# The last LayerNorm of a hybrid decoder layer: two engines on row block 6, the variance constant on DVE, the last store on ACT's queue

## The chip, the cores and the metric

The kernel runs on one core of one Trainium2 chip. The metric is device time in microseconds (us), median of three runs. The engines are called as the profile calls them: PE (matmul; PEld is its weight load), DVE (vector), ACT (scalar), POOL (GpSimd) and SP, which issues most DMAs. A "q" behind a name (SPq, POOLq) is the engine's instruction queue: DMA issues, semaphores, drains.

## What is computed

One decoder layer in float32 on 1024 rows of width 1024. Its end, on which the change bears most, is

```python
h = layer_norm(DEEPNORM_ALPHA * h + mix, ln1_g[l], ln1_b[l])
h = layer_norm(DEEPNORM_ALPHA * h + memory_cross_attention(h, mem, ...), ln2_g[l], ln2_b[l])
h = layer_norm(DEEPNORM_ALPHA * h + swiglu_ffn(h, ffn_w_gate_up[l], ffn_w_down[l]), ln3_g[l], ln3_b[l])
```

with `layer_norm` being, per row, `(x - mean) * rsqrt(var + 1e-5) * g + b`. `mix` is the output of an S5 state-space group and a differential attention group.

## The kernel before, in words

The 1024 rows are eight row blocks of 128 rows, one block being a tile `u` of 128 partitions by 1024 columns. Most matmuls are done as three in a rounded format (`fp32r`), on a high and a low part of each operand; making these parts costs ACT and DVE much work along the whole kernel. The stages follow each other: input LayerNorm and projections, S5, attention, output projection with the first LayerNorm (`project`, eight blocks), cross attention with the second LayerNorm (`project` again, eight blocks, woven with the last of the cross attention), the gate and up product (`gate_up`), and the down product (`down`).

Statistics of these three LayerNorms come from `ln_stats` (line 310), called 24 times, eight times per LayerNorm. Two `bn_stats` and one `bn_aggr` on DVE give mean and variance (tile `bmv`). Line 317 adds the constant 1e-5 to the variance on POOL (tile `bv`). Line 307 takes the power -0.5 of that on POOL (tile `lny`). The caller then goes on, on DVE.

`project` (line 1088) normalises its block on DVE, and `resid` (line 320) does two 128x1024 products and sums of the block on POOL, back to back, and stores the result.

`down` (line 1402) works in two halves of four row blocks. Blocks 0 to 3 are finished while PE works on the second half. For blocks 4 to 7 the last five of the 22 steps of the sum are done block by block and half by half, and each half of 512 columns is added to the residual on DVE (`stt`, reading PSUM). The PSUM tiles are, in the order of the blocks, `sc`, `sc`, `mm`, `tp`: the tile `tp` is block 7. After each block comes `tail(ti, z, fast)` (line 1426) with `fast` being 0, 2, 1, 2 for blocks 4, 5, 6, 7:

- `fast` 0 (block 4): a small DVE instruction makes `nm`, ACT normalises the block, DVE multiplies with `g3`, POOL adds `b3`, POOL's queue stores.
- `fast` 1 (block 6): the same, but DVE also adds `b3`, and SP's queue stores.
- `fast` 2 (blocks 5 and 7): no ACT. For each half of columns DVE does `(z - mean) * g3`, which needs only `bmv`, then `z * rstd + b3`, which needs `lny`, and SP's queue stores the half.

The order of each engine's instructions is not written out by hand: the framework's planner takes instructions by priority (place in the program) and by a simulated time line, and each engine then runs its list in order. At the end of the program (line 1617) each engine drains, SP waits for all transfers and engines, and a barrier ends the run.

The trace puts nearly all instructions on line 120, that of a helper, so they are told apart by tile names.

Of the kernel before, what the change touches and what calls it, by code (L numbers as in the profile page):

```python
# [12 lines left out]
ALU = mybir.AluOpType  # L13
# [12 lines left out]
EPS = 1e-5  # L26
# [66 lines left out]
def layer(ctx: ExitStack, tc: tile.TileContext, a, out, dbg=None):  # L93
# [55 lines left out]
    sc_e, ve, po, pe, sy = (Eng(getattr(nc, n), n) for n in ("scalar", "vector", "gpsimd", "tensor", "sync"))  # L149
# [22 lines left out]
    def U(shape=(128, 1024), dt=F32):  # L172
        return alloc("u", 1024, shape, dt)

    def H(shape=(128, 512), dt=F32):
        return alloc("h", 512, shape, dt)

    def fr_(*ts_):
        for t in ts_:
            if isinstance(t, (tuple, list)):  # L180
                fr_(*t)
            else:
                _, tag, nm, slot = held.pop(id(t))
                free[tag].append((slot, used.pop(nm), cur[0], icnt[0], last.get(nm, 0)))
# [19 lines left out]
    def S(w, name, dt=F32):  # L204
        return sm.tile([128, w], dt, tag=name, name=name)
# [7 lines left out]
    def act(o, i, scale=1.0, bias=0.0, func=None, accum=None):  # L213
        f = func or (AF.Copy if isinstance(bias, float) and bias == 0.0 else AF.Identity)
        kw = {}
        if not (isinstance(bias, float) and bias == 0.0):
            kw["bias"] = bias
        if accum is not None:
            kw["accum_out"] = accum
        return sc_e.activation(out=o, in_=i, func=f, scale=scale, **kw)  # L220

    def tt(e, o, x, y, op):
        return e.tensor_tensor(out=o, in0=x, in1=y, op=op)

    def ts(e, o, x, s1, op0, s2=None, op1=None):
        if op1 is None:
            return e.tensor_scalar(out=o, in0=x, scalar1=s1, scalar2=None, op0=op0)
        return e.tensor_scalar(out=o, in0=x, scalar1=s1, scalar2=s2, op0=op0, op1=op1)

    def stt(o, x, s, y, op0, op1):  # L230
        return ve.scalar_tensor_tensor(out=o, in0=x, scalar=s, in1=y, op0=op0, op1=op1)
# [5 lines left out]
    def lo_of(o, x, hi, e=None):  # L237
        return tt(e or ve, o, x, hi.bitcast(F32), ALU.subtract)
# [16 lines left out]
    def load(ap, shape=(128, 1024)):  # L255
        t = U(shape)
        sy.dma_start(out=t, in_=ap)
        return t
# [4 lines left out]
    def wload(ap, shape=(128, 1024), e=None, eh=None):  # L263
        raw = load(ap, shape)
        w = split(raw, shape, None, e, eh)
        fr_(raw)
        return w
# [37 lines left out]
    def rsqrt(v, w, nm):  # L305
        y = S(w, nm + "y")
        tt(po, y, v, half_[:, 0:w], ALU.pow)
        return y

    def ln_stats(z):  # L310
        st = S(12, "bst")
        for c in range(2):
            ve.bn_stats(out=st[:, 6 * c:6 * c + 6], in_=z[:, 512 * c:512 * c + 512])
        mv = S(2, "bmv")
        ve.bn_aggr(out=mv, in_=st)
        v = S(1, "bv")
        ts(po, v, mv[:, 1:2], EPS, ALU.add)
        return mv[:, 0:1], rsqrt(v, 1, "ln")

    def resid(z, g, b, dst):  # L320
# [6 lines left out]
    def row_bc(n):  # L327
        t = U()
        ap = a["rows"]
        sy.dma_start(out=t, in_=bass.AP(tensor=ap.tensor, offset=ap.offset + n * DM, ap=[[0, 128], [1, DM]]))  # L330
        return t
# [756 lines left out]
    def project(src, wname, r_idx, grow, gn, bn, hT, r_out, at=None):  # L1088
# [4 lines left out]
        for i in range(NT):  # L1093
# [14 lines left out]
            if i == NT - 1:  # L1108
                fr_(w)
            mean, rstd = ln_stats(z)  # L1110
            ts(ve, z, z, mean, ALU.subtract, rstd, ALU.mult)
            resid(z, g, b, r_dram[r_out][i])
# [289 lines left out]
    def down():  # L1402
        g3, b3 = row_bc(6), row_bc(7)
        bk = [x[:, 512 * c:512 * c + 512] for x in banks["sc"] for c in range(2)] + banks["mm"] + banks["tp"]
        tails = []

        def prep(half, j):
            w = wload(a["wdown"][j])
            hx = U([128, 2, 512], F32R)
            v = H()  # L1410
            sy.dma_start(out=v, in_=hid_dram[j, half])
            act(hx[:, 0, :], v)
            lo_of(hx[:, 1, :], v, hx[:, 0, :])
            fr_(v)
            return w, hx

        def go(j, w, hx, i, cs=(0, 1)):
            s = slice(128 * i, 128 * i + 128)
            for c in cs:
                n = slice(512 * c, 512 * c + 512)  # L1420
                o = bk[2 * i + c]
                pe.matmul(o, lhsT=hx[:, 0, s], rhs=w[0][:, n], start=(j == 0), stop=False)
                pe.matmul(o, lhsT=hx[:, 0, s], rhs=w[1][:, n], start=False, stop=False)
                pe.matmul(o, lhsT=hx[:, 1, s], rhs=w[0][:, n], start=False, stop=(j == NJ - 1))

        def tail(ti, z, fast=0):
            mean, rstd = ln_stats(z)
            if fast < 2:
                nm = S(1, "nm3")
                stt(nm, mean, -1.0, rstd, ALU.mult, ALU.mult)  # L1430
                act(z, z, scale=rstd, bias=nm)
                tt(ve, z, z, g3, ALU.mult)
                tt(ve if fast else po, z, z, b3, ALU.add)
                (sy if fast else po).dma_start(out=out[128 * ti:128 * ti + 128, :], in_=z)
                fr_(z)
                return
            for c in range(2):
                n = slice(512 * c, 512 * c + 512)
                stt(z[:, n], z[:, n], mean, g3[:, n], ALU.subtract, ALU.mult)
                stt(z[:, n], z[:, n], rstd, b3[:, n], ALU.mult, ALU.add)  # L1440
                sy.dma_start(out=out[128 * ti:128 * ti + 128, n], in_=z[:, n])
            fr_(z)

        ahead = [prep(0, j) for j in range(DD)]
        for half in range(2):
            for j in range(NJ - LAST):
                w, hx = ahead.pop(0)
                if j + DD < NJ - LAST:
                    ahead.append(prep(half, j + DD))
                for i in range(4):  # L1450
                    go(j, w, hx, i)
                fr_(w, hx)
                if tails and j % 3 == 2:
                    tail(*tails.pop(0))
            zs = [load(r_dram[2][4 * half])]
            last = [prep(half, j) for j in range(NJ - LAST, NJ)]
            if half == 0:
                ahead = [prep(1, j) for j in range(DD)]
            for i in range(4):
                ti = 4 * half + i  # L1460
                if i < 3:
                    zs.append(load(r_dram[2][ti + 1]))
                z = zs[i]
                for c in range(2):
                    for jj in range(LAST):
                        go(NJ - LAST + jj, last[jj][0], last[jj][1], i, (c,))
                    n = slice(512 * c, 512 * c + 512)
                    stt(z[:, n], z[:, n], ALPHA, bk[2 * i + c], ALU.mult, ALU.add)
                if half == 0:
                    tails.append((ti, z))  # L1470
                else:
                    tail(ti, z, (0, TA, 1, 2)[i])
            fr_(last)
# [147 lines left out]
```

## Time and profile before

| what | value |
|---|---|
| three runs | 1528.99, 1529.14, 1533.43 us; median 1529.14 |
| profiled execution | 1530.15 us, span 1528.4 us |
| PE busy | 1424.2 us (93%), 7246 matmuls |
| DVE busy | 918.2 us (60%), 1507 instructions |
| ACT busy | 526.8 us (34%) |
| POOL busy | 494.3 us (32%) |
| mean granted PE clock | 0.972 of full |

The span is the time from the first to the last instruction in the trace; 1.75 us of the profiled execution lie outside of it. The shares are averages over stages with different limits. In the last slice of the page (the last 38 us) PE is busy for six tenths and POOL for nearly none.

### The profile page before, as it was taken

To read this page: it belongs to the slowest core of one execution; us is meant where nothing else is said; L and a number is where in the kernel's file an instruction comes from. 1 tells how busy PE (TensorE), PEld (TensorE's weight loads), DVE (VectorE), ACT (ScalarE), POOL (GpSimd) and SP (SyncE) were. 2 spreads that over 40 slices of the span, in tenths; PEclk is the share of its full clock that TensorE was granted. 3 is DMA by queue.
4 is the path that set the end of the run, shared out by engine and by line. 5 is a ranking of instruction groups with operands and counts; after the bars stand their busy time and mean duration, and the time that the engine had idled before them with its cause. 6 is when DMAs were issued, how large, how long until landed. Compare 5 with 4: busy or idle time off the path is not lost.

```text
span 1528.4 us, 18806 instructions
## 1 busy us (share of the span) xinstructions
PE 1424.2 (93%) x7246; PEld 1201.2 (79%) x7246; DVE 918.2 (60%) x1507; ACT 526.8 (34%) x926; POOL 494.3 (32%) x414
## 2 busy tenths in 40 slices
PE   7988779999896999999999899999999999999996
PEld 6988668878776788888887678878888887888885
DVE  8896665566785465635557856656555547337305
ACT  5411214655774012425212533323323326324200
POOL 4344431132004766000255645534444420004002
PEclk9999889999998899999999999999999999999998
DMA  9104361221337124124222223312222249554401
GB/s 343 68 1 97 75 159 42 56 56 51 116 101 285 42 69 153 48 76 129 93 83 83 97 90 117 111 69 84 89 83 82 84 148 330 190 185 146 152 28 55
DMA packets 53870, 166.82 MB, mean 109 GB/s; under 512 B 6346, under 2 KB 10863, under 8 KB 53780
## 3 DMA queue, kind: packets, MB, share of 16 engines
q1 hardware_dynamic: 41652, 124.17, 24.7%
q0 software_dynamic: 9232, 30.94, 5.9%
q10 hardware_dynamic: 2896, 10.51, 2.7%
q8 instruction: 57, 0.93, 0.3%
q14 instruction: 33, 0.27, 0.1%
HBM read 126.77 MB, written 34.62 MB: 106 GB/s over the span
## 4 chain that ended last, share of the span: by engine, by line
PE 63%; DVE 13%; DMA 10%; issue 5%; POOL 4%; ACT 3%; SPq 0%; ACTq 0%; POOLq 0%; DVEq 0%
PE mm L120 33%; PE sc L120 23%; DVE u L120 11%; PE tp L120 7%; POOL u L120 3%; ACT u L120 3%; DMA u<-in_wgu_dram 2%; DMA kr<-u 2%; DMA u<-in_x_dram 1%; DMA u<-in_wkvv_dram 1%; DVE h L120 1%; DMA u<-kr 1%; DMA hidd<-u 1%; DMA u<-in_wqk_dram 1%; ACT h L120 1%
## 5 line engine op out<-in xcount | busy, mean ns | idle before, releaser
L120 PE MATMUL mm<-u,u 128*128 128x512 f32 (+1 forms) x3288 | 729.1, 372 | 34.5 <-ACT u L120 19.7
L120 PEld LDWEIGHTS mm<-u,u 128*128 128x128 f32 x3288 | 570.4, 192 | 140.6 <-ACT u L120 22.2
L120 PE MATMUL sc<-u,u 128*128 128x512 f32 (+4 forms) x2744 | 598.6, 375 | 25.6 <-DVE u L120 8.1
L120 PEld LDWEIGHTS sc<-u,u 128*128 128x128 f32 (+2 forms) x2744 | 482.6, 200 | 114.6 <-ACT u L120 10.8
L120 DVE TENSOR_TENSOR u<-u,u 128x1024 fp32r<-128x1024 f32 (+5 forms) x257 | 317.2, 1253 | 209.1 <-ACT u L120 171.6
L120 ACT ACTIVATE u<-u 128x1024 fp32r<-128x1024 f32 (+1 forms) x200 | 195.0, 985 | 467.8 <-DMA u<-in_wgu_dram 118.5
L120 POOL TENSOR_TENSOR u<-u,u 128x512 f32<-128x512 f32 (+4 forms) x155 | 298.1, 1930 | 123.1 <-DVE u L120 43.8
L120 PE MATMUL tp<-u,u 128*128 128x512 f32 (+3 forms) x600 | 105.6, 319 | 1.5 <-ACT u L120 1.5
L120 POOL TENSOR_SCALAR bv<-bmv 128x1 f32<-128x1 f32 x24 | 7.8, 326 | 286.2 <-DVE bmv L120 286.0
L120 PEld LDWEIGHTS tp<-u,u 128*128 128x128 f32 (+1 forms) x600 | 85.8, 176 | 14.4 <-ACT u L120 2.8
L120 PE MATMUL tp<-eye,u 128*128 128x128 f32 x424 | 65.5, 285 | 22.9 <-DVE u L120 18.7
L120 ACT ACTIVATE u<-mm 128x512 fp32r<-128x512 f32 (+3 forms) x84 | 48.0, 572 | 92.6 <-PE mm L120 87.2
L120 POOL TENSOR_TENSOR u<-u 128x512 f32<-128x512 f32 x26 | 46.0, 1769 | 102.1 <-DMA u<-in_wgu_dram 72.2
L120 PEld LDWEIGHTS tp<-eye,u 128*128 128x128 f32 x424 | 52.1, 146 | 32.0 <-DVE u L120 19.9
L120 DVE TENSOR_TENSOR u<-h,u 128x512 fp32r<-128x512 f32 (+1 forms) x92 | 69.1, 773 | 5.9 <-ACT u L120 5.0
L120 ACT ACTIVATE u<-tp 128x512 f32<-128x512 f32 (+2 forms) x76 | 40.4, 557 | 79.1 <-PE tp L120 70.7
L120 DVE SCALAR_TENSOR_TENSOR u<-u,mm 128x512 f32<-128x512 f32 x36 | 24.6, 684 | 61.1 <-PE mm L120 57.5
L120 ACT ACTIVATE u<-sc 128x512 f32<-128x512 f32 (+2 forms) x61 | 31.6, 542 | 50.1 <-PE sc L120 42.5
L120 ACT ACTIVATE h<-tp,pp 128x512 f32<-128x512 f32 x40 | 29.6, 775 | 47.2 <-PE tp L120 36.3
L120 DVE TENSOR_TENSOR u<-mm,u 128x512 fp32r<-128x512 f32 (+2 forms) x44 | 27.9, 637 | 29.7 <-ACT u L120 29.5
L120 POOL TENSOR_SCALAR u<-u 128x1024 fp32r<-128x1024 f32 x14 | 15.5, 1105 | 92.3 <-DMA u<-in_wqk_dram 59.7
L120 DVE BATCH_NORM_STATS2 bst<-u 128x6 f32<-128x512 f32 x64 | 43.3, 686 | 1.3
(175 smaller groups left out, 899.6 us busy)
## 6 DMA issues: line engine op xcount, KB each, us to landing
u<-in_wgu_dram SPq DMA_DIRECT2D x52, 512.0 KB, 4.1
u<-in_wdown_dram SPq DMA_DIRECT2D x44, 512.0 KB, 4.6
h<-hidd SPq DMA_DIRECT2D x44, 256.0 KB, 4.2
u<-in_x_dram SPq DMA_DIRECT2D x16, 512.0 KB, 7.0
rd<-u POOLq DMA_DIRECT2D x16, 512.0 KB, 3.3
u<-rd SPq DMA_DIRECT2D x16, 512.0 KB, 3.5
hidd<-h POOLq DMA_DIRECT2D x22, 256.0 KB, 2.3
hidd<-u POOLq DMA_DIRECT2D x22, 256.0 KB, 3.3
```

Source lines behind the costliest of these rows:

```text
L120: ins = f(*args, **kw)
```

## The change

Three edits. In `ln_stats` the constant is added to the variance by DVE, for all 24 calls. In `tail` with `fast` 1 (block 6 alone) the multiplication with `g3` and the addition of `b3` are each done for columns 0 to 639 on DVE and for columns 640 to 1023 on POOL. In `tail` with `fast` 2 (blocks 5 and 7) the store of the second half of columns is issued from ACT's queue; the first half stays on SP's.

```diff
--- before.py
+++ after.py
@@ -314,7 +314,7 @@
         mv = S(2, "bmv")
         ve.bn_aggr(out=mv, in_=st)
         v = S(1, "bv")
-        ts(po, v, mv[:, 1:2], EPS, ALU.add)
+        ts(ve, v, mv[:, 1:2], EPS, ALU.add)
         return mv[:, 0:1], rsqrt(v, 1, "ln")
 
     def resid(z, g, b, dst):
@@ -1429,8 +1429,13 @@
                 nm = S(1, "nm3")
                 stt(nm, mean, -1.0, rstd, ALU.mult, ALU.mult)
                 act(z, z, scale=rstd, bias=nm)
-                tt(ve, z, z, g3, ALU.mult)
-                tt(ve if fast else po, z, z, b3, ALU.add)
+                if fast:
+                    for e, n in ((ve, slice(0, 640)), (po, slice(640, 1024))):
+                        tt(e, z[:, n], z[:, n], g3[:, n], ALU.mult)
+                        tt(e, z[:, n], z[:, n], b3[:, n], ALU.add)
+                else:
+                    tt(ve, z, z, g3, ALU.mult)
+                    tt(po, z, z, b3, ALU.add)
                 (sy if fast else po).dma_start(out=out[128 * ti:128 * ti + 128, :], in_=z)
                 fr_(z)
                 return
@@ -1438,7 +1443,7 @@
                 n = slice(512 * c, 512 * c + 512)
                 stt(z[:, n], z[:, n], mean, g3[:, n], ALU.subtract, ALU.mult)
                 stt(z[:, n], z[:, n], rstd, b3[:, n], ALU.mult, ALU.add)
-                sy.dma_start(out=out[128 * ti:128 * ti + 128, n], in_=z[:, n])
+                (sc_e if c else sy).dma_start(out=out[128 * ti:128 * ti + 128, n], in_=z[:, n])
             fr_(z)
 
         ahead = [prep(0, j) for j in range(DD)]
```

## Rows read from the trace of the kernel before

**Rows 1.** Stretches: from:to us, length, then busy us of each engine, clock, DMA.
```profile
800.00:840.00 40.00, 38.07 (x175) 31.00 (x174) 29.45 (x33) 10.80 (x14) 22.90 (x17) 1.00 0.22 79
...
840.00:880.00 40.00, 33.07 (x145) 25.52 (x144) 33.22 (x27) 22.59 (x31) 24.92 (x16) 0.96 0.28 92
...
1390.00:1490.00 100.00, 100.00 (x443) 82.83 (x442) 39.34 (x41) 26.68 (x33) 12.46 (x8) 1.00 0.37 119
```

**Rows 2.** Line 1617, the program's end: ns min/median/max, first to last start us.
```profile
L1617 POOLq DRAIN  x1: 9641/9641/9641, 1517.9 to 1517.9; - x1
...
L1617 SPq DRAIN  x2: 7/7/7, 1522.7 to 1522.8; - x2
```

**Rows 3.** Time line of POOL, blocks 6 and 7: start us, us, what [idle before <-releaser].
```profile
1509.88 0.61 POOL L120 TENSOR_SCALAR bv<-bmv 128x1 f32<-128x1 f32 x1 [1.04 <-DVE bmv L120]
1510.58 0.91 POOL L120 TENSOR_TENSOR lny<-bv,half 128x1 f32<-128x1 f32 x1
1517.13 0.77 POOL L120 TENSOR_SCALAR bv<-bmv 128x1 f32<-128x1 f32 x1 [5.64 <-DVE bmv L120]
1517.99 0.93 POOL L120 TENSOR_TENSOR lny<-bv,half 128x1 f32<-128x1 f32 x1
```

**Rows 4.** Time line of DVE, from block 6's statistics to the last instruction.
```profile
1509.58 0.21 DVE L120 BATCH_NORM_AGGREGATE bmv<-bst 128x2 f32<-128x12 f32 x1
1509.71 1.36 DVE L120 SCALAR_TENSOR_TENSOR u<-u,lny,u 128x512 f32<-128x512 f32 x2
1511.52 0.16 DVE L120 SCALAR_TENSOR_TENSOR nm<-bmv,lny 128x1 f32<-128x1 f32 x1 [0.45 <-POOL lny L120]
...
1512.99 2.48 DVE L120 TENSOR_TENSOR u<-u,u 128x1024 f32<-128x1024 f32 x2
1515.40 0.68 DVE L120 SCALAR_TENSOR_TENSOR u<-u,tp 128x512 f32<-128x512 f32 x1
...
1516.84 0.21 DVE L120 BATCH_NORM_AGGREGATE bmv<-bst 128x2 f32<-128x12 f32 x1
1517.08 1.41 DVE L120 SCALAR_TENSOR_TENSOR u<-u,bmv,u 128x512 f32<-128x512 f32 x2
1518.95 1.42 DVE L120 SCALAR_TENSOR_TENSOR u<-u,lny,u 128x512 f32<-128x512 f32 x2 [0.46 <-POOL lny L120]
```

**Rows 5.** Time line of PE and of ACT, their last instructions.
```profile
1506.73 6.96 PE L120 MATMUL tp<-u,u 128*128 128x512 f32 x30
...
1511.72 1.24 ACT L120 ACTIVATE u<-u,nm,lny 128x1024 f32<-128x1024 f32 x1 [9.07 <-DVE nm L120]
```

**Rows 6.** Groups by form, DVE: operation, count | busy us, mean ns | idle before.
```profile
L120 DVE TENSOR_SCALAR cmx<-cmx 128x2 f32<-128x2 f32 x16 | 2.4, 163 | 0.1
...
L120 DVE SCALAR_TENSOR_TENSOR nm<-xmv,xrs 128x1 f32<-128x1 f32 x4 | 1.7, 422 | 0.5 <-POOL xrs L120 0.5
```

**Rows 7.** Time line of POOL and DVE while `resid` runs in the second `project`.
```profile
796.85 5.25 POOL L120 TENSOR_TENSOR u<-u,u 128x1024 f32<-128x1024 f32 x2 [0.99 <-DVE u L120]
...
795.90 0.81 DVE L120 TENSOR_SCALAR u<-u,bmv,lny 128x1024 f32<-128x1024 f32 x1 [1.00 <-POOL lny L120]
...
797.08 2.77 DVE L120 TENSOR_TENSOR u<-h,u 128x512 fp32r<-128x512 f32 x1
799.76 2.62 DVE L120 CAST u<-h 128x512 fp32r<-128x512 f32 x1
```

**Rows 8.** Time line of POOL and DVE around one power, first `project`.
```profile
570.37 0.99 POOL L120 TENSOR_TENSOR lny<-bv,half 128x1 f32<-128x1 f32 x1
...
570.24 0.69 DVE L120 TENSOR_TENSOR u<-h,u 128x512 fp32r<-128x512 f32 x1
570.85 0.42 DVE L120 CAST u<-h 128x512 fp32r<-128x512 f32 x1
```

**Rows 9.** Time line of the queues: a store from ACT's, the two last from SP's.
```profile
39.95 0.33 ACTq L120 DMA_DIRECT2D ktd<-u  x1
...
1519.73 0.99 SPq L120 DMA_DIRECT2D out_dram<-u  x2
```

## The prediction

> **What bounds the kernel now.** I read first the busy time by stretches, then the end of the program, then the time lines of single engines over the last 20 us. By stretches PE is the bound nearly everywhere: from 1390 to 1490 it is busy for 100.00 of 100 us, and the four blocks finished there (blocks 0 to 3 of the last LayerNorm) cost nothing [rows 1]. From 800 to 840 PE is idle for 1.93 us and from 840 to 880 for 6.93 us [rows 1]; there the second `project` runs, and DVE and POOL set the pace.
>
> The end is not set by the last store. SP has seen all transfers and drains at 1522.8, while POOL's drain starts at 1517.95 and lasts 9.64 us, to 1527.59; everything else in the program's end comes after that [rows 2]. POOL's last instruction, the power of block 7, ends at 1518.92 [rows 3], so the drain ends 8.67 us behind it. No row says what the drain does in these 8.67 us. I take it as a fixed price behind POOL's last instruction: what counts at the end is when `lny` of block 7 is finished, and the last DVE pass, to 1520.37 [rows 4], and both its stores have 4.8 us of cover.
>
> PE's last matmul ends at 1513.69 [rows 5], but the addition that reads it starts only at 1515.40: DVE is still at the two passes of block 6 [rows 4]. So the path at the end is: power of block 6, `nm` at 1511.52, additions and passes on DVE to 1515.40, statistics of block 7 to 1517.05, constant and power on POOL to 1518.92, drain.
>
> **How DVE and POOL get in each other's way.** Two stretches decide most of the sum. While POOL does its two 128x1024 instructions from 796.85, a DVE instruction of a form that takes 0.69 us at 570.24 takes 2.77 us, and the cast behind it 2.62 us against 0.42 us at 570.85 [rows 7, 8]. The times fit strict turns: DVE's first instruction gets through when POOL's first is done (797.08 + 2.77 - 0.69 = 799.16, that is 2.31 us after POOL's start), POOL's second when that one is done, and the cast after POOL's second. The small POOL instructions wait too: the constant of block 6 ends at 1510.49, just behind the first half of DVE's pair of 1.36 us (about 1510.40), and the power at 1511.49, 0.42 us behind the pair's end at 1511.07; block 7 is the same with 1517.90 and, 0.43 us behind 1518.49, 1518.92 [rows 3, 4].
>
> **The constant on DVE, blocks 6 and 7.** The nearest rows for the DVE instruction are 0.163 us (128x2) and, as the upper end, 0.422 us [rows 6]. I take the first, which is the same operation, and 0.03 for the gap: 0.19 us.
>
> Block 6: DVE's pair begins 0.19 later, at 1509.90, its first half ends at 1510.58; the power, now alone on POOL, gets its turn there and needs 0.42 us more: 1511.00. The pair ends at 1511.26, and `nm` starts at 1511.29 instead of 1511.52: -0.23 us. It is then the pair that is late, no longer POOL.
>
> Block 7: from the end of `bmv` the power ends today after 1518.92 - 1517.05 = 1.87 us. After the change: 0.03 + 0.19, then the first half of the pair, 0.70, then 0.43: 1.35 us, so -0.52 us. Ends: if the power waits for both halves, 0.22 + 1.41 + 0.43 = 2.06, +0.19; if it gets in ahead of them, 0.22, 0.09 for the signal and 0.42, 0.73: -1.14.
>
> In that step the power must not hold DVE up for its 0.42 us. At 570.37 it ran behind a DVE instruction that ended at 570.93 and ended itself at 571.36, 0.43 us later; the cast on DVE meanwhile took its plain 0.42 us, from 570.85 to 571.27 [rows 8]. So by this row DVE goes on beside a power. The Trainium skill says otherwise ("SBUF — State Buffer", section "Who interferes with whom"): whichever of the two engines gets the shared port pair first holds it for the whole instruction, and the other fully blocks. By that rule the second half of each pair would come 0.42 us later, and `nm` of block 6 at 1511.71; it is the third rival.
>
> **Block 6 divided by columns.** Today: two instructions, from 1512.99 to the next one's start at 1515.40, 2.41 us [rows 4]. By 0.69 us for 512 and 1.24 us for 1024 columns [rows 4, 8], 640 columns cost DVE 0.83 us. POOL's part by 2.31 us per 1024 columns [rows 7] is 0.87 us for 384. If both engines ran side by side, DVE would be free after 2 x 0.83 - 0.07 = 1.59 us, -0.82 us. But all four instructions read two tiles, as those of [rows 7] do, so they take turns. With DVE first: 0.83 + 0.87 + 0.83 - 0.07 = 2.46 us, +0.05. With POOL first: 0.87 + 0.83 + 0.87 + 0.83 - 0.07 = 3.33 us, +0.92. Who is first is close: ACT releases both at 1511.72 + 1.24 = 1512.96 [rows 5], DVE started 0.03 us behind that [rows 4], and POOL starts 0.09 us behind what releases it (1509.79 to 1509.88) [rows 3, 4]. I take DVE first, +0.05. POOL's second part then ends about 1516.3, before the power of block 7 is due at 1517. The store of block 6, on SP, waits for it, some 0.9 us later than today; behind it on SP only the store of block 7 is queued, due three us later.
>
> **The last store on ACT's queue.** An issue costs 0.33 us on ACT's queue, and 0.33 us on SP's by the pair (1519.73 to 1520.72, the second waiting for its data until 1520.37) [rows 9]. SP is free when the data come, and ACT has nothing behind it. Between 0 and 0.05 us either way, hidden under POOL's drain; without that cover the same. I take 0.
>
> **The constant in the two `project` stages, 16 times.** It takes 0.30 us off POOL's way (constant and gap) and puts 0.19 us on DVE's: the wait of DVE of 1.00 us ahead of 795.90 [rows 7] becomes 0.89. The first eight lie under a busy PE. I count -0.1 us for the one or two that lie on the path between 795 and 880. Ends: 16 x -0.11 = -1.8 us, and, at 0.422 us each, 16 x 0.12 = +1.9 us.
>
> **Sum.** -0.23 + 0.05 - 0.52 = -0.70 at the end, -0.1 before it: -0.8 us on the profiled execution (span 1528.4, 1530.15 with the 1.75 us around it). The median of the runs is 1.01 us below that execution, so 1529.14 - 0.8 = 1528.3 us.
>
> **Rivals.**
> - *POOL first at block 6.* +0.92 in place of +0.05: 1529.2 us. For it: 0.06 us decide, and DVE is still at the statistics that end at about the same time. Against: today's start at 1512.99.
> - *The drain does not follow the power*, its end being set by something older on POOL. Then only -0.1 stays: 1529.0 us. No row excludes it; that POOL's list ends with the power speaks against it.
> - *The port is held for the whole power* (the page's rule above): block 6's `nm` +0.19 in place of -0.23, sum -0.38: 1528.8 us. Against it stands the one cast in [rows 8].
> - *Slower: new collisions in the second `project`.* The planner orders the lists anew when an instruction changes engine, and 24 do, from the first `project` on. Place: 795 to 880, where PE already waits [rows 1]. Price: a pair of `resid` instructions that catches a DVE instruction and a cast costs DVE 2.08 + 2.20 = 4.28 us [rows 7, 8]. One more such pair gives 1532.6, two 1536.9; it decides from the second on. For it: DVE is the path there. Against: the planner's costs move by tenths only, and a long delay needs POOL to start just ahead of DVE, as it did by 0.23 us at 796.85.
> - *Faster: one such collision less*, 1528.3 - 4.3 = 1524.0 us. The power comes 0.11 us earlier, which moves the pair of `resid` against DVE's list; the same close order, the other way.
>
> **How the numbers follow.** Chances: forecast 0.42, POOL first 0.17, drain 0.08, port held 0.10, slower by collisions 0.13 (0.05 for one pair, 0.08 for two or more), faster 0.10. A measurement of this kernel can tell about 0.3%, 4.6 us, from no change: below 1524.6 is faster, above 1533.7 slower. The first four cases and one pair more are no change by that, 0.82; one collision less is faster, 0.10; two pairs more slower, 0.08. The range goes from one collision less, 1523.9, to one more, 1532.8, and holds the bounds of the unknown prices (-1.8 and +1.9 in the `project` stages, +0.92 and +0.19 at the end); outside lies mostly the case of two pairs.
>
> **What would show it.** Right: `bv` on DVE at about 0.16 us; `lny` of blocks 6 and 7 ending about 0.4 us behind the first half of DVE's pair; `nm` about 0.2 us earlier against PE's last matmul; at block 6 the four instructions in turns, one of DVE's two lengthened by about 0.9 us; the addition of the last `tp` half some 1.5 us behind PE's end as now; POOL's drain still ending 8.7 us after `lny`, and the stores landed more than 4 us before it. Wrong: passes of block 6 that overlap at full speed; a drain of another length; a time that moves by 4 us or more, which by this account can come only from 795 to 880.

## The result, and the profile after

The changed kernel takes 1538.81 us (median of 16 runs, 1535.83 to 1544.16) against 1529.78 us (16 runs of the kernel before beside it): a ratio of 1.0058, 95% interval 1.0044 to 1.0071. It is about 9.0 us slower. The forecast was 1528.3 us and its range ended at 1532.8 us, so both missed. The profiled execution of after took 1535.83 us, 5.7 us more than the profiled one of before; that of after lies 3.0 us below its median, so one pair of executions is not enough, and further down the stages are compared over several kernels. Of the executions of the experiments one, of e7, took 3608 us and is left out of its ratio.

The page of after (span, then busy time of each engine):

```profile
span 1534.0 us, 18793 instructions
...
PE 1426.5 (93%) x7246; PEld 1202.9 (78%) x7246; DVE 928.0 (60%) x1531; ACT 527.5 (34%) x926; POOL 490.5 (32%) x392
```

DVE is busy for 9.8 us more than before, with 24 instructions more; POOL for 3.8 us less. Nothing on this page says where 9 us went. For that I cut the span at instructions that every kernel has: the powers of the LayerNorms (`lny`), the stores `hidd<-h` of `gate_up`, PE's last matmul. Each number is the time between two starts in one profiled execution, in the last row from the end of the matmul.

| stretch, us | before | after |
|---|---|---|
| first `project`, 1st to 8th power | 78.80 | 83.31 |
| from there to the 9th power | 150.91 | 152.85 |
| second `project`, 9th to 16th power | 85.53 | 86.18 |
| 16th power to first `hidd<-h` | 69.25 | 69.21 |
| first to second `hidd<-h` | 21.38 | 24.08 |
| PE's last matmul to the end of the span | 14.71 | 14.05 |

These are +4.5, +1.9, +0.7, +2.7 and -0.7 us, together 9.1. The stretches left out give 3.4 us back in this one pair of executions; they differ by about 2.5 us between executions of one and the same order (`gate_up`'s sixth to ninth `hidd<-h`: 56.1 to 58.7 in the order of before), so nothing is read from them.

How sure the stretches are is told by the traces of the experiments below. In seven kernels the order ahead of `down` is that of before (before, e2, e6 and e7 change nothing there, e8, e11 and e12 hold it), in four it is the new one (after, e1, e9, and e10 with one instruction moved):

| stretch, us | order of before | new order |
|---|---|---|
| first `project`, 1st to 8th power | 77.41 to 79.51 | 83.14 to 84.29 |
| from there to the 9th power | 150.81 to 151.23 | 152.07 to 153.09 |
| second `project`, 9th to 16th power | 85.19 to 85.87 | 85.29 to 86.48 |
| 16th power to first `hidd<-h` | 67.36 to 69.25 | 68.09 to 70.57 |
| first to second `hidd<-h` | 21.34 to 21.92 | 24.05 to 24.13 |

In all these executions the first two and the last lie apart; the second `project` and the stretch behind it overlap.

**The tail came out as predicted in sum, by other steps.** DVE in after, around blocks 6 and 7:

```profile
1515.00 1.40 DVE L120 SCALAR_TENSOR_TENSOR u<-u,lny,u 128x512 f32<-128x512 f32 x2
...
1517.04 0.21 DVE L120 BATCH_NORM_AGGREGATE bmv<-bst 128x2 f32<-128x12 f32 x1
1517.17 0.65 DVE L120 SCALAR_TENSOR_TENSOR u<-u,tp 128x512 f32<-128x512 f32 x1
1517.73 0.15 DVE L120 TENSOR_SCALAR bv<-bmv 128x1 f32<-128x1 f32 x1
1518.63 0.16 DVE L120 SCALAR_TENSOR_TENSOR nm<-bmv,lny 128x1 f32<-128x1 f32 x1
...
1520.11 0.83 DVE L120 TENSOR_TENSOR u<-u,u 128x640 f32<-128x640 f32 x1 [1.31 <-ACT u L120]
1520.85 0.68 DVE L120 SCALAR_TENSOR_TENSOR u<-u,tp 128x512 f32<-128x512 f32 x1
1521.45 1.02 DVE L120 TENSOR_TENSOR u<-u,u 128x640 f32<-128x640 f32 x1
...
1523.11 0.21 DVE L120 BATCH_NORM_AGGREGATE bmv<-bst 128x2 f32<-128x12 f32 x1
1523.35 0.15 DVE L120 TENSOR_SCALAR bv<-bmv 128x1 f32<-128x1 f32 x1
1523.42 1.40 DVE L120 SCALAR_TENSOR_TENSOR u<-u,bmv,u 128x512 f32<-128x512 f32 x2
```

POOL in after, the same stretch, then its drain and PE's last group:

```profile
1518.04 0.56 POOL L120 TENSOR_TENSOR lny<-bv,half 128x1 f32<-128x1 f32 x1 [3.25 <-DVE bv L120]
1520.15 3.17 POOL L120 TENSOR_TENSOR u<-u,u 128x384 f32<-128x384 f32 x2 [1.55 <-ACT u L120]
1523.58 0.99 POOL L120 TENSOR_TENSOR lny<-bv,half 128x1 f32<-128x1 f32 x1 [0.27 <-DVE bv L120]
...
L1622 POOLq DRAIN  x1: 9689/9689/9689, 1523.5 to 1523.5; - x1
...
1512.99 6.96 PE L120 MATMUL tp<-u,u 128*128 128x512 f32 x30
```

The reader is to see four things. The power of block 7 ends at 1524.57, and POOL's drain 8.6 us later, as in [rows 2, 3]. From the end of block 7's `bmv` (1523.32) to the end of that power is 1.25 us, against 1.87 before; forecast 1.35. DVE came first at block 6, by 0.04 us (1520.11 against 1520.15). And the planner moved more than the diff: the second pass of block 5 and an addition of a `tp` tile now stand ahead of block 6's `bv`, and the last `tp` addition stands between the two passes of block 6.

### The profile page after: what moved, and what is told of

Read it like the earlier page. It is cut to its first block, busy times and chain, and to the rows that moved or that the text cites. A ratio compares the mean times of both kernels' runs of the same rounds, so it can differ in the third digit from the quotient of the medians.

```text
span 1534.0 us, 18793 instructions
## 1 busy us (share of the span) xinstructions
PE 1426.5 (93%) x7246; PEld 1202.9 (78%) x7246; DVE 928.0 (60%) x1531; ACT 527.5 (34%) x926; POOL 490.5 (32%) x392
## 4 chain that ended last, share of the span: by engine, by line
PE 50%; DVE 4%; POOL 2%; DMA 1%; issue 1%; ACT 1%; DVEq 0%; POOLq 0%; ACTq 0%; SPq 0%
PE sc L120 26%; PE mm L120 20%; DVE u L120 4%; PE tp L120 4%; POOL u L120 2%; ACT u L120 1%; DMA u<-in_wdown_dram 0%; DMA u<-in_wgu_dram 0%; DMA u<-in_wo_dram 0%; DMA u<-in_wq_dram 0%; DMA hidd<-u 0%; DVE bst L120 0%; POOL lny L120 0%; POOL rd L120 0%; ACT h L120 0%
## 5 line engine op out<-in xcount | busy, mean ns | idle before, releaser
L120 DVE TENSOR_TENSOR u<-u,u 128x1024 fp32r<-128x1024 f32 (+6 forms) x257 | 315.5, 1247 | 207.9 <-ACT u L120 162.9
L120 POOL TENSOR_TENSOR u<-u,u 128x512 f32<-128x512 f32 (+5 forms) x157 | 301.1, 1924 | 128.1 <-DVE u L120 47.0
L120 POOL TENSOR_TENSOR lny<-bv,half 128x1 f32<-128x1 f32 x24 | 15.4, 641 | 293.7 <-DVE bv L120 293.7
L120 DVE TENSOR_TENSOR u<-h,u 128x512 fp32r<-128x512 f32 (+1 forms) x92 | 77.5, 867 | 6.5 <-ACT u L120 5.6
L120 ACT ACTIVATE u<-h 128x512 fp32r<-128x512 f32 (+1 forms) x60 | 35.6, 651 | 26.5 <-PE tp L120 10.1
```

The costliest lines, as they stand in the source:

```text
L120: ins = f(*args, **kw)
```

## The experiments

All ratios are to the kernel before, run beside them, with 95% intervals; medians are of the same session.

### Which edit costs the time

e1 is the kernel before with one word changed, for all 24 calls; e2 has the other two edits; e3 and e4 put the constant on DVE in one `project` stage alone.

```diff
 e1:  -ts(po, v, mv[:, 1:2], EPS, ALU.add)      +ts(ve, v, mv[:, 1:2], EPS, ALU.add)
 e2:  the changed kernel with                    ts(po, v, mv[:, 1:2], EPS, ALU.add)
 e3, e4: the kernel before; ln_stats(z, e=None) has ts(e or po, v, mv[:, 1:2], EPS, ALU.add), and project calls
 e3:  +mean, rstd = ln_stats(z, ve if r_out == 1 else po)   # constant on DVE in the first project
 e4:  +mean, rstd = ln_stats(z, ve if r_out == 2 else po)   # constant on DVE in the second project
```

> Kernel before with only the variance constant on DVE, all 24 times; row block 6 and the last store as before. Theory A (new order): the planner orders DVE, POOL, ACT and PE anew from the first LayerNorm of the two project stages on, and the new order lets DVE instructions run into POOL's 128x1024 pairs; so nearly all of the loss is here: 7 to 10 us over the kernel before (about 1538), PE's last matmul 5 to 7 us later, DVE waits of 2 us and more at the first project around 550 to 570. Rival B (the instruction itself): 24 times 0.15 us more on DVE, so +3.7 us at most, and no new wait of PE. Rival C (the end of the kernel): the loss lies behind PE's last matmul, from block 6 divided between two engines; then this kernel stays within 1 us of the kernel before.

> Kernel after with the constant back on POOL: only row block 6 divided by columns and the last store from ACT's queue. Theory A: within 1.5 us of the kernel before, as the order of all earlier work is that of before; block 6 costs DVE about as long as before (turns with POOL). Rival B: the same, within 1 us. Rival C: +5 to +9 us, behind PE's last matmul.

> Kernel before with the constant on DVE in the first project alone (8 times); constant on POOL in the second project and at the end. Theory A: +4 to +7 us, with the PE gap of about 1.8 us near 568 and a lower granted clock behind it as in the kernel after. Rival B: 8 times 0.15 us at most, +1.2 us. Rival C: 0.

> Kernel before with the constant on DVE in the second project alone (8 times). Until 740 us the order of work is that of the kernel before. Theory A: a loss of 2 to 5 us between 800 and 960, through other collisions of DVE with POOL there; the sign is less sure than for the first project, since a new order can also lose collisions. Rival B: +1.2 us at most. Rival C: 0.

| run | us | before | ratio |
|---|---|---|---|
| e1 | 1538.99 | 1529.10 | 1.0056 [1.0034, 1.0077] |
| e2 | 1527.62 | 1529.10 | 0.9988 [0.9974, 1.0001] |
| e3 | 1534.95 | 1529.10 | 1.0036 [1.0020, 1.0051] |
| e4 | 1533.02 | 1529.10 | 1.0020 [1.0007, 1.0032] |

The constant is the whole loss, and the two stages add up: 5.9 and 3.9 us make 9.8, e1 lost 9.9 (each with an interval of some 2 to 3 us to either side). In e3 the first `project` takes 83.84 us, in e4 78.77; the 24 us between the first two `hidd<-h` stand in e4 (23.68), not in e3 (21.60).

### The instruction, or the order of the lists

The planner made new lists for every engine. With the constant on DVE, 817 of the 6875 places in PE's list (as recorded in the kernels of e8 and e9) hold another instruction than before, though no matmul is touched; in DVE's list, the constants left out, it is 132 of 1443. e8 has the instruction without the new order, e9 the new order without the instruction. Each engine's list is held by edges from each instruction to its neighbours in a recorded list (only the lines that add the edges are shown):

```diff
+k = int(ins.ins.name[2:]); made[k] = ins.ins
+if PREV.get(k) in made:
+    tc.add_manual_dep(ins.ins, made[PREV[k]].name, nosync, reason="order")
+if NEXT.get(k) in made:
+    tc.add_manual_dep(made[NEXT[k]], ins.ins.name, nosync, reason="order")
 e8: e1 with the lists of before;  e9: before with the lists of e1
```

> The constant on DVE all 24 times, but every engine's list is held to the order of the kernel before (each instruction made to follow its predecessor in that order; the constant sits right behind its bn_aggr on DVE). Block 6 and last store as before. Theory A (the new order costs, not the instruction): the loss goes, within 1.5 us of the kernel before, about 1528 to 1530.5. Rival B (the instruction on DVE itself, or the longer way to the power): the loss of about 10 us stays, 1537 to 1540.

> The kernel before, with the constant on POOL right ahead of its power, but every engine's list held to the order that the planner makes when the constant is on DVE. Theory A: slower by 8 to 11 us though no instruction has changed engine, with the PE gap near 568 and the lengthened DVE instructions. Rival B: within 1.5 us of the kernel before.

e8: 1527.10 against 1529.21 us, 0.9985 [0.9975, 0.9996]. e9: 1539.16 against 1529.21, 1.0062 [1.0045, 1.0079]. So the order costs the time, and the instruction itself costs nothing; it gains some 2 us (by the interval 0.6 to 3.8). First `project`: 78.88 us in e8, 84.29 in e9.

**What the new order does in the first `project`.** Windows of before, then of after (from:to, length, busy us of PE, PEld, DVE, ACT, POOL, PE clock, DMA share, GB/s):

```profile
545.00:600.00 55.00, 55.00 (x260) 45.77 (x259) 37.23 (x50) 10.63 (x13) 41.06 (x30) 1.00 0.31 109
...
570.00:580.00 10.00, 10.00 (x50) 8.35 (x49) 9.14 (x12) 2.51 (x3) 7.16 (x5) 1.00 0.39 141
```

```profile
545.00:600.00 55.00, 53.17 (x243) 43.50 (x242) 42.34 (x52) 10.05 (x12) 36.38 (x23) 0.97 0.25 91
...
560.00:570.00 10.00, 8.17 (x40) 6.46 (x40) 9.50 (x10) 2.27 (x4) 6.07 (x4) 0.99 0.09 34
...
570.00:580.00 10.00, 10.00 (x43) 8.21 (x42) 9.11 (x14) 2.51 (x3) 4.31 (x3) 0.84 0.41 152
```

PE waits 1.83 us, and in the ten us behind that gap its granted clock is 0.84 on average, between its two levels of 1.2 and 2.4 GHz, instead of 1.00. It gets 43 matmuls done there, where before gets 50 done at 1.00. At 0.21 us each (55.00 us for 260 in before) these seven are worth 1.5 us, so gap and clock make an estimated 3.3 of the 4.5 us; where the rest went is not shown. DVE's groups by form in the same 55 us say why (count | busy us, mean ns | idle before). Before:

```profile
L120 DVE CAST u<-h 128x512 fp32r<-128x512 f32 x8 | 7.4, 928 | 0.6 <-ACT h L120 0.6
...
L120 DVE TENSOR_TENSOR u<-h,u 128x512 fp32r<-128x512 f32 x8 | 5.4, 687 | 0.1
```

After:

```profile
L120 DVE TENSOR_TENSOR u<-h,u 128x512 fp32r<-128x512 f32 x8 | 11.8, 1476 | 0.2
L120 DVE CAST u<-h 128x512 fp32r<-128x512 f32 x8 | 8.5, 1068 | 0.2 <-ACT h L120 0.2
```

The same eight instructions take 11.8 us instead of 5.4. Pairs of `resid` met DVE before, too, but other instructions of it; in sum DVE is busy for 5.1 us more in these 55 us (42.34 against 37.23). After's time lines show what the eight meet, POOL and DVE and then PE:

```profile
552.92 4.94 POOL L120 TENSOR_TENSOR u<-u,u 128x1024 f32<-128x1024 f32 x2 [0.64 <-DVE u L120]
...
563.41 4.96 POOL L120 TENSOR_TENSOR u<-u,u 128x1024 f32<-128x1024 f32 x2 [1.90 <-DVE u L120]
...
555.65 2.76 DVE L120 TENSOR_TENSOR u<-h,u 128x512 fp32r<-128x512 f32 x1
...
563.18 2.95 DVE L120 CAST u<-h 128x512 fp32r<-128x512 f32 x2
566.05 2.87 DVE L120 TENSOR_TENSOR u<-h,u 128x512 fp32r<-128x512 f32 x1
568.84 0.68 DVE L120 SCALAR_TENSOR_TENSOR u<-u,mm 128x512 f32<-128x512 f32 x1
...
569.57 4.38 PE L120 MATMUL mm<-u,u 128*128 128x512 f32 x11 [1.83 <-DVE u L120]
```

It is the pattern of [rows 7] in the stage where I had not looked for it. The pair of `resid` on POOL from 563.41 lies beside two casts and a product of DVE that take 5.82 us where 2 x 0.42 + 0.69 = 1.53 would do by [rows 8]: 4.3 us. DVE's next addition starts only at 568.84, and PE, which waits for it, has by then used up the work it had in hand and stood for 1.83 us. The Trainium skill ("SBUF — State Buffer", section "Who interferes with whom") states that a DVE instruction with two SBUF inputs contends with a GpSimd instruction that reads SBUF. The trace agrees for the product, with 2.87 us against 0.69. The two casts, which have one input, are lengthened as well, to 2.95 us against 0.84.

### One instruction moved, and the pairs cut short

e10 is e1 with its lists held, except that in DVE's list one addition that frees a matmul (`u<-u,mm`) goes ahead of the two casts and the product. e13 and e14 cut the `resid` pairs of the first `project` from 1024 to 64 columns and store the unscaled block (so scale and shift of that copy are left out), once in the new order and once in the old; e15 and e16 do it in both `project` stages. e13 and e15 have the constant on DVE, e14 and e16 on POOL.

```diff
 e13 to e16, resid:
-tt(po, r, z, g, ALU.mult); tt(po, r, r, b, ALU.add)
+m = slice(0, 64 if short else 1024)       # short: r_out == 1 (e13, e14), always (e15, e16)
+tt(po, r[:, m], z[:, m], g[:, m], ALU.mult); tt(po, r[:, m], r[:, m], b[:, m], ALU.add)
-po.dma_start(out=dst, in_=r)
+po.dma_start(out=dst, in_=z if short else r)
```

> The constant on DVE 24 times in the planner's own new order (1538.99 us when run earlier), held, with one instruction of DVE's list moved: in the first project the addition that empties the PSUM tile mm for the first half of the sixth row block (u<-u,mm) goes ahead of the two casts and the subtraction that wait for POOL's resid pair, instead of behind them, as it stands in the order of the kernel before. Theory A, sharpened: PE's gap of 1.8 us near 568 comes from this addition being queued behind instructions that wait for POOL's port, and the low granted clock (0.83) of the 10 us behind it from the gap; so the gap goes and the first project gets 3 to 3.5 us shorter: 6 to 7 us over the kernel before instead of 10. Rival F (the gap comes from DVE being busy as such, or from another instruction of the list): gap and time stay, 9 to 10.5 us over before.

> Constant on DVE, the planner's new order held, but in the first project POOL's two resid instructions work on 64 columns instead of 1024 and the unscaled block is stored (scale and shift of the residual copy of the first LayerNorm are left out). Theory A (port turns with POOL's pairs): the first project, from its first power to its eighth, takes 78 to 79.5 us as in the old order instead of 83.1 to 84.3, and the whole is 4 to 6 us over the kernel before instead of 10. Rival G (the new lists are worse in themselves): 83 us and 9 to 11 us over before.

> The control: the kernel before in its own order, held, with the same resid instructions of the first project on 64 columns (the same scale and shift left out). PE is busy throughout this stage in the old order, so both theories expect no gain there: within 1.5 us of the kernel before.

> As e13_new_short, with resid cut to 64 columns in both project stages (scale and shift of both residual copies left out). Theory A: against e16_old_short_both only 0 to 3 us slower, where the full kernels differ by 10. Rival G: still 8 to 10 us slower than it.

> The control of e15_new_short_both: the kernel before in its own order, held, resid cut to 64 columns in both project stages (the same left out). From 795 to 880 us PE waits for DVE, and DVE for POOL's pairs, so a gain of 2 to 7 us over the kernel before by theory A; by rival G 0 to 2 us.

| run | order, pairs cut in | us | before | ratio | first `project` |
|---|---|---|---|---|---|
| e10 | new, one moved; none | 1538.08 | 1527.39 | 1.0073 [1.0054, 1.0092] | 83.97 |
| e13 | new; first | 1533.04 | 1528.25 | 1.0025 [1.0010, 1.0040] | 77.22 |
| e14 | old; first | 1528.11 | 1528.25 | 0.9997 [0.9985, 1.0009] | 77.46 |
| e15 | new; both | 1529.20 | 1528.25 | 1.0003 [0.9988, 1.0019] | 76.79 |
| e16 | old; both | 1523.90 | 1528.25 | 0.9973 [0.9959, 0.9988] | 77.80 |

e10 missed: the gap at 569 was gone, but the loss stayed. Its DVE and PE, ten us later:

```profile
578.93 2.76 DVE L120 TENSOR_TENSOR u<-h,u 128x512 fp32r<-128x512 f32 x1
581.62 2.58 DVE L120 CAST u<-h 128x512 fp32r<-128x512 f32 x1
...
585.57 12.82 PE L120 MATMUL mm<-u,u 128*128 128x512 f32 x48 [3.19 <-DVE u L120]
```

The next pair does the same, and PE waits 3.19 us there. So moving one instruction is not enough: DVE falls behind by some 4 us in each of these two pairs, and PE stands where DVE has not caught up.

e13 and e14 show that the pairs cause the loss in this stage. With short pairs the new order's first `project` takes 77.22 us, 6 less, and the old one's 77.46. DVE and POOL of e13, and the window:

```profile
564.40 0.89 DVE L120 CAST u<-h 128x512 fp32r<-128x512 f32 x2
565.20 0.81 DVE L120 TENSOR_TENSOR u<-h,u 128x512 fp32r<-128x512 f32 x1
...
564.63 0.83 POOL L120 TENSOR_TENSOR u<-u,u 128x64 f32<-128x64 f32 x2 [0.99 <-DVE u L120]
...
550.00:605.00 55.00, 55.00 (x261) 45.75 (x260) 33.44 (x55) 12.09 (x16) 21.08 (x27) 1.00 0.37 123
```

The casts take 0.89 us instead of 2.95, the product 0.81 instead of 2.87, PE is busy for all 55 us at a clock of 1.00. (Short pairs also leave POOL free earlier, 21.08 us busy here; that DVE's instructions themselves get shorter is what speaks for the sharing.)

e15 against e16 missed its expectation of 0 to 3 us: with all pairs short the new order is still 5.3 us slower by the medians (1529.20 - 1523.90), 4.6 by the ratios, where the intervals leave room for an estimated 1 to 8. That lies between the two theories. About half of the loss therefore does not come from the pairs that were cut; POOL has other instructions, in `gate_up` too, and no run tells whether these play a part.

Where the rest lies: in one execution each, 1.5 us between the `project` stages (153.84 against 152.35), 0.9 in the second one, and 2.4 us between the first two `hidd<-h` (23.99 against 21.63). The first of these is mostly a shift of the mark between two stretches, the eighth power. From the first power to the ninth, both stretches together, e15 takes 230.63 us and e16 230.15, e13 231.24 and e14 229.43; with full pairs it is 228.6 to 230.5 us in the order of before and 236.2 to 237.1 in the new one. So up to the ninth power short pairs take the loss from some 7 us to between 0.5 and 1.8. From the 16th power to the first `hidd<-h` e15 is 3.3 us longer than e16 (68.86 against 65.60), in a stretch that varies by 1.9 us within the order of before.

There is one more wait that only the new order has, on PE in after:

```profile
612.55 0.74 PE L120 MATMUL sc<-u,u 128*128 128x256 f32 x4 [0.90 <-ACT u L120]
```

It is also in e1, e3 and e9 (0.93 to 1.44 us) and in no kernel of the old order. But e10, e13 and e15 do not have it, and e10 takes 153.09 us from the eighth power to the ninth all the same, so it does not explain that stretch.

### Whose list carries the rest

In `gate_up`'s first group after shows this on PE and ACT:

```profile
905.13 5.60 PE L120 MATMUL sc<-u,u 128*128 128x512 f32 x24
912.25 0.73 PE L120 MATMUL sc<-u,u 128*128 128x512 f32 x2 [1.52 <-ACT u L120]
...
913.85 2.58 PE L120 MATMUL sc<-u,u 128*128 128x512 f32 x10 [0.40 <-DVE u L120]
...
924.72 0.73 PE L120 MATMUL sc<-u,u 128*128 128x512 f32 x2 [0.58 <-ACT u L120]
...
910.14 0.63 ACT L120 ACTIVATE u<-u 128x512 fp32r<-128x512 f32 x1 [3.45 <-PE sc L120]
```

And before:

```profile
895.78 8.55 PE L120 MATMUL sc<-u,u 128*128 128x512 f32 x37
904.17 0.62 PE L120 MATMUL mm<-u,u 128*128 128x512 f32 x2
...
901.02 0.63 ACT L120 ACTIVATE u<-u 128x512 fp32r<-128x512 f32 x1 [4.62 <-PE sc L120]
```

ACT's instruction waits for an `sc` product. Before, PE still had matmuls until 904.33 when ACT started at 901.02; after, it had them only until 910.73 when ACT started at 910.14, and the three waits sum to 2.5 us, the size of the loss in that stretch. To see whose list does it, e17 has the new lists but PE's of before, and e18 the lists of before but PE's new one; both have the constant on DVE.

> The constant on DVE in all 24 LayerNorm statistics, the new order of instructions on DVE, POOL, ACT and SP, but PE's list held to the order of the kernel before. Theory PE: where the new order moves matmuls (a block's last product and its transposes nearer to the end of PE's list), PE has nothing left to do while it waits for ACT or DVE; that is the loss in gate_up's first group (24.1 us against 21.5) and between the two projects (152.5 to 153 against 151). Then both go back to the old values here, the first project keeps its 83 us, and the time is 1.0025 to 1.0035 of before. Theory of the other lists: the two stages are lost through ACT's and DVE's order; then they stay at 24.1 and 152.5 or more and the time is 1.005 to 1.006 of before.

> The constant on DVE in all 24, the lists of DVE, POOL, ACT and SP held to the order of before, PE's list in the new order. Theory PE: gate_up's first group 24.1 us, between the projects 152.5 to 153, first project near 78.5 as before; the time 1.001 to 1.002 of before (e8, the same with PE's old list, was 0.9985). Theory of the other lists: 21.5, 151 and 78.5, and 0.998 to 0.9995 of before. A first project above 82 us here would mean that the collisions on the port too come from PE's list.

e17: 1548.52 against 1529.82 us, 1.0126 [1.0104, 1.0149]. e18: 1550.22, 1.0140 [1.0120, 1.0159]. Both theories missed the time by far: each mixture is slower than either plan whole. A list that was planned beside others does not fit different ones. One point is clean: the first `project` takes 85.92 us in e17 and 79.38 in e18, so its loss goes with the lists of DVE, POOL, ACT and SP, which e17 has new together, and not with PE's. Between the first two `hidd<-h` e17 has 22.04 and e18 24.85 us, as the theory of PE's list would have it, but e17's PE waits 2.19 us for DVE in that same place, so that is a hint and no proof. Between the `project` stages both are at 156 to 158 us, and nothing is told apart.

### The tail by itself

e6 makes the whole change, but takes the constant to DVE in the last LayerNorm alone. e7 takes the power of block 7 off POOL in the kernel before:

```diff
 e6, in tail:                    e7, in ln_stats, block 7 alone:
+mean, rstd = ln_stats(z, ve)    +ts(ve, v, mv[:, 1:2], EPS, ALU.add)
                                 +act(sd, v, func=AF.Sqrt)
                                 +ve.reciprocal(out=r, in_=sd)
```

> The change confined to the last LayerNorm: constant on DVE for its 8 calls, block 6 divided, last store from ACT's queue; the constant of both project stages stays on POOL, so the order of work until then is that of before. Theory A: 0.5 to 2 us faster than the kernel before (the divided block alone, run earlier, was 1.5 us faster, and the constant lets the last power end some 0.5 us sooner). Rival C (the end of the kernel costs): slower by 1 us or more.

> The kernel before, but block 7's rstd is made without POOL: constant on DVE, square root on ACT, reciprocal on DVE. POOL's last instruction is then the power of block 6, which ended at 1511.5. Theory D (the end is POOL's drain, 8.7 us behind POOL's last instruction): the drain ends near 1520.2, ahead of the last store; the store then sets the end, and DVE's second pass starts some 0.4 us earlier: 4 to 5.5 us faster. Rival E (the drain's end hangs on something else, a DMA from POOL's queue or the last store): 0 to 0.5 us faster.

e6: 1530.25 against 1529.21 us, 1.0001 [0.9990, 1.0013]; its tail is 14.09 us. The expected gain of 0.5 to 2 us is not shown: the interval goes from 1.5 us faster to 2.0 slower. e7: 1525.81 against 1529.21 us, 0.9977 [0.9963, 0.9991]. The end of e7:

```profile
1509.77 0.92 POOL L120 TENSOR_TENSOR lny<-bv,half 128x1 f32<-128x1 f32 x1
...
L1623 POOLq DRAIN  x1: 9622/9622/9622, 1509.7 to 1509.7; - x1
L1623 SPq DRAIN  x3: 7/7/7, 1521.7 to 1521.9; - x3
...
1517.67 0.16 DVE L120 RECIPROCAL rs<-sd 128x1 f32<-128x1 f32 x1
1517.87 1.42 DVE L120 SCALAR_TENSOR_TENSOR u<-u,rs,u 128x512 f32<-128x512 f32 x2
```

POOL's last instruction is now block 6's power, to 1510.69, and the drain still ends 8.6 us behind it, at 1519.3. SP's wait for the stores, at 1521.9, is the later one now. The tail falls from 14.71 to 9.62 us, 5.1; the runs show 3.4, with an interval from 1.4 to 5.7. That the drain is a price behind POOL's last instruction, which the prediction could only take as given, is shown by this for a last instruction that is a 128x1 power, the only kind in these kernels.

### The order kept, and a faster version

e12 is the whole change with before's lists up to block 6's last statistics. e11 is e8 with e7's edit.

> The whole change (constant on DVE 24 times, block 6 divided, last store from ACT's queue), with every engine's list held to the order of the kernel before up to block 6's last statistics; the few instructions after that are placed by the planner. Theory A: the forecast of the prediction comes back, 0.5 to 2.5 us faster than before. Rival B or C: slower.

> Constant on DVE 24 times in the order of the kernel before (2.1 us faster than before when run earlier), and block 7's rstd by ACT and DVE without POOL (3.4 us faster when run earlier, alone); block 6 and the last store as before. If both gains are real and in different places: 4 to 6.5 us faster than the kernel before. If they overlap at the end of the kernel (the first one's gain is POOL's earlier last power): 3 to 4.5 us.

e12: 1526.77 against 1527.39 us, 1.0001 [0.9986, 1.0015], the tail at 13.34 us. The loss is gone; the expected gain of 0.5 to 2.5 us is not shown, as the interval reaches 2 us to either side. e11: 1522.93 against 1527.39, 0.9978 [0.9966, 0.9991]; its tail is 9.32 us. e11 beats both kernels: 4.5 us below before by the medians, 3.4 by the ratio (interval 1.4 to 5.2). Whether its two gains add up or overlap is not told apart by that.

## Why the prediction was wrong, step by step

- **The constant in the two `project` stages (-0.1): the step that failed.** "The first eight lie under a busy PE" stands there without a row, and nothing was said of how far DVE is ahead of PE. PE was indeed busy for 55.00 of 55 us there, but a busy PE covers a loss on DVE only by as much as DVE is ahead of it, and one pair takes 4.3 us from DVE. Measured: +9.9 us in e1, 5.9 of it with the first eight calls, the ones that I had counted at nothing. I had costed the instruction, 0.11 us at a time, where the cost was in the new order (e8, e9). Its upper end was also mis-added, though that decides nothing: with the gap of 0.03 us, which the lower end has, it is 16 x 0.15 = 2.4 us and not 1.9.
- **The rival of new collisions (0.13)** had the mechanism and the price of a pair, 4.28 us against 4.3 measured, but the wrong place: from the 9th power to the first `hidd<-h`, which holds 795 to 880, 0.6 us were lost, in the first `project` 4.5. Its argument against itself, that the planner's costs move by tenths only, is refuted: tenths were enough to change 817 places in PE's list. So is the sign that a move of 4 us or more can come only from 795 to 880. And about half of the loss stays when the pairs are cut short (e15, e16), so it is not a collision with them.
- **`nm` of block 6 (-0.23): wrong.** It came 1.32 us ahead of PE's last matmul's end, 2.17 before: 0.85 us later, since other DVE work was put ahead of `bv`. The power took 0.56 us with no pair in its way.
- **Block 6 divided (+0.05): right in its parts** (DVE first, 0.83 us for 640 columns; the times fit turns with POOL, whose two parts take 3.17 us). Neither of DVE's two was lengthened by 0.9 us, the second took 1.02, since the planner put the last `tp` addition between the passes, 0.90 us behind PE's end instead of 1.71. This step and the one on `nm` together gave 0.0 where -0.18 was forecast: block 7's statistics end 3.37 us behind PE's end, as before (3.36).
- **Block 7's power (-0.52): right**, -0.62. That the port is not held for the whole power is borne out, against the third rival: the pair at 1523.42 takes 1.40 us beside the power at 1523.58, as the pair at 1518.95 without one, 1.42 [rows 4].
- **The drain, and the last store at 0: right**; the drain ended 8.6 us behind the power, and e7 shows that it sets the end, which comes 5.1 us earlier without the power of block 7. The store by itself was not tried. Tail in sum: -0.66, forecast -0.70; that they agree so well is luck, as the steps on `nm` and block 6 were off and the power made up for part of it.
- **Open:** what the new order costs apart from these pairs, some 5 us: 2.4 us in `gate_up`'s first group, where the trace shows PE out of work ahead of an ACT instruction and the list that does it is not settled; 0.5 to 1.8 us up to the ninth power and about 0.9 in the second `project`, without a cause found; and the rest in stretches that vary by about as much between executions of one order.

## What to carry to other kernels

Where a planner makes the lists, moving one small instruction to another engine is a change of every list: compare the lists before pricing the instruction, and hold the old order when the local gain is what is wanted. A stage in which PE is busy all the time hides only what DVE is ahead of it, so look at DVE's slack and at which POOL instructions run beside it. At the end of a program, ask which engine's drain comes last; here it was worth more (e7, 0.9977) than all three edits with the old order held (e12, 1.0001).

## What the hardware showed that was not expected

Lists from two plans cost 19 to 20 us when they are crossed (e17, e18), twice the loss of the new plan by itself. And POOL's drain ends 8.6 to 8.7 us behind its last instruction, which is a 128x1 power each time (before 8.67, after 8.6, e7 8.6, though another power is the last there): taking one power away from POOL's end gave 3.4 us (e7).
